# Half of a modulation group on VectorE, three modulation groups by halves at three norms, and VectorE's tiles loaded by GpSimd

## The chip, the cores and the metric

The kernel runs on one core of a Trainium2 chip. The metric is the device time of one execution in microseconds (us); the median of the runs of a kernel stands for it. A core has five engines that run their own instruction streams in order: TensorE (PE: matmuls), VectorE (DVE), ScalarE (ACT), GpSimd (POOL) and SyncE (SP). They wait for each other by semaphores. Transfers are issued from a queue of SP, ACT or POOL and are moved by 16 DMA engines. In a timeline a row of an issue stands under SPq, ACTq or POOL.

## The reference

Two blocks follow each other on 512 latent tokens of width 1024 (and 256 context tokens in the first block). The first block has two layers; each is modulated by six vectors for the latents and six for the context, which come from a condition `c` by one product with `ada_w`:

```python
sc_lat, sc_ctx = jax.nn.silu(c), jax.nn.silu(c_ctx)
for i in range(2):
    mod_l = (sc_lat @ ada_w[i] + ada_b[i])[:, None, :]
    mod_c = sc_ctx @ ada_w[i] + ada_b[i]
    sh1_l, s1_l, g1_l, sh2_l, s2_l, g2_l = jnp.split(mod_l, 6, axis=-1)   # mod_c alike
    h = rms_norm(x, norm1_g[i]) * (1 + s1) + sh1
    x = x + g1 * mixer(h)          # i = 0: gated linear attention; i = 1: neighbourhood attention
    h = rms_norm(x, norm2_g[i]) * (1 + s2) + sh2
    x = x + g2 * conv_ffn(h)       # i = 1: the latents alone
x = second_block(rms_norm(x_lat, final_g))
```

The second block (two layers of three attention branches and an MLP) isn't touched by the change.

## The kernel before

**Modulation groups.** The twelve vectors of the two layers are computed in six groups of two vectors, 0 to 5, each for latents and context at once; a group is a product of 2 x 1024 (the silu of the conditions, `scT`) with 1024 x 2048 weights (`ada_w`, 8 MB in f32). Each group is needed at its own time: group 0 at the very start, group 1 for the output projection of the gated attention and the first feed-forward's norm, group 2 for that norm's scales and the feed-forward's output, 3 and 4 for the second layer's attention, 5 for the second layer's feed-forward.

There are two ways of computing a group. `gada` (L355) takes PE: 16 steps (eight slices of 128 rows, two halves of 1024 columns), each loads 512 KB into a tile `aw` and multiplies it in two matmuls of 512 columns with the 32 columns of `scT` as the stationary operand, so that the four blocks of 512 columns land in four groups of 32 partitions of the tile `ad`. At its end a DVE transpose and a sum with the bias give `mod`. `vada` (L386) takes DVE: it loads tiles `at` of 128 x 512 (256 KB, two buffers), multiplies each by a scalar for each partition and adds it to an accumulator `aa` (one operation for the latents, one for the context; L406 for the first slice, L408 for the others), and PE sums over the partitions at the end of each half with a matrix `unit` (L416).

Before the change: group 0 by its own function on PE in the start; 1 and 2 by `gada` in the gated attention, as a side work that is dealt out one step for each 2.5 units of planned main work (`AEV`), loads on SP's queue through four buffers; 3 and 4 by `vada` in the first feed-forward, loads on SP's queue; 5 by `gada` in two pieces at the first and the second norm, where PE waits for a norm anyway, loads on ACT's queue through seven buffers (`ADA5`: two steps ahead of each norm, six behind it).

**Stages.** The start loads the tokens and sums their squares over the features (`sumsq`: ACT squares, DVE adds, L479), which gives 1/rms (`rstd`: a matmul with ones, L351, then two ACT operations). `modulate0` (L514) then makes `hh` (on ACT) and the low part `hl` (DVE subtracts `hh` from `E`, which POOL makes, L521). All main products are three matmuls of rounded high and low parts (`mm3`: L330, L332, L334). The first projections follow, then v (L639 to L641), then four heads of the gated attention; PE is given projections of the next head between the parts of a head. The output projection and the first norm (`token_rstd`, `modulate`) come next, the first feed-forward (`ffn`), the second norm, the neighbourhood attention (`na`) with its output projection, the third norm and the second feed-forward.

**What sets the order.** The code is written in program order with generators: `weave` and `mixed` (L229, L241) deal out steps of side work by planned costs. A scheduler then places the instructions of each engine in a fixed stream by its own estimate of when each can run; it may move an instruction ahead of ones that were written earlier. On the chip each engine runs that stream in order and waits at the head of it. A tile with n buffers can be loaded anew only when the readers of the n-th tile before it are done.

## Time and profile before

| | us |
|---|---|
| median of 3 runs | 3698.85 (3698.39 to 3700.05) |
| profiled execution | 3697.38 |
| its span | 3695.6 |
| PE busy | 3617.4 (98%) |
| DVE busy | 2175.7 (59%) |
| ACT busy | 1434.2 (39%) |
| POOL busy | 361.7 (10%) |

The span runs from the first to the last instruction of the profiled execution. The windows that the rows use are: the start up to the first v projection at 60.64, from there to the first level of head 0 at 84.87, and three heads from first product of a head to that of the next (84.87, 186.75, 286.58, 371.85). The first norm lies at 496 to 512, the second at 1076 to 1085, the third at 1452 to 1460.

### The profile page before, as it was taken

The page shows a single profiled execution, that of the slowest core. Times are in us where ns is not written, and L with a number is a line of the kernel's source. Part 1 is how long each engine was busy: PE and PEld are TensorE (multiplying, and loading weights), DVE is VectorE, ACT ScalarE, POOL GpSimd, SP SyncE. Part 2 cuts the span into 40 slices and gives each one's busy share as a digit, 9 for nine tenths or more (in the row PEclk, how much of TensorE's full clock was granted, in tenths as well). Part 3 has the DMA queues.
Part 4 walks back from the last instruction along what each step waited for, and adds up shares of the span by engine and source line. Part 5 has one row for each costly group of instructions (what it writes and reads, how often), then busy time and mean ns, then how long its engine had stood idle before and what let it go on. Part 6 is the DMA issues. An engine that isn't in the chain of part 4 may idle for free.

```text
span 3695.6 us, 48674 instructions
## 1 busy us (share of the span) xinstructions
PE 3617.4 (98%) x19296; PEld 2972.7 (80%) x19296; DVE 2175.7 (59%) x3471; ACT 1434.2 (39%) x2199; POOL 361.7 (10%) x342
## 2 busy tenths in 40 slices
PE   7999999999999998999999999999999999999998
PEld 5778878888878886888787877888888787788888
DVE  5566776364355776444766775544456687644446
ACT  4334432121344454333546534422234653432223
POOL 2000000000001110000210121210121012121011
PEclk9999999999999999999999999999999999999999
DMA  6332343232112222323322232323332223233323
GB/s 254 123 95 66 120 151 107 71 117 83 60 62 58 52 57 66 99 95 99 116 82 87 92 102 80 120 97 97 97 119 82 91 89 104 81 120 98 97 94 118
DMA packets 128931, 360.21 MB, mean 97 GB/s; under 512 B 31664, under 2 KB 33968, under 8 KB 128704
## 3 DMA queue, kind: packets, MB, share of 16 engines
q1 hardware_dynamic: 97632, 321.70, 27.1%
q10 hardware_dynamic: 28928, 27.47, 2.6%
q0 software_dynamic: 2144, 7.93, 0.6%
q8 instruction: 152, 2.49, 0.3%
q14 instruction: 75, 0.61, 0.1%
HBM read 342.10 MB, written 8.65 MB: 95 GB/s over the span
## 4 chain that ended last, share of the span: by engine, by line
PE 45%; DVE 3%; issue 1%; ACT 1%; POOL 0%; DMA 0%; SPq 0%; DVEq 0%; POOLq 0%; ACTq 0%
PE mm L330 13%; PE mm L334 13%; PE mm L332 13%; PE yp L1335 1%; DVE wlo L320 1%; PE yp L1426 1%; PE mm L1238 1%; PE ma L1495 1%; PE mm L1240 0%; PE mm L1239 0%; PE ma L1414 0%; DMA tf<-s 0%; POOL ta L1483 0%; DVE ta L1478 0%; PE ma L1398 0%
## 5 line engine op out<-in xcount | busy, mean ns | idle before, releaser
L319 ACT ACTIVATE whi<-wst 128x1024 fp32r<-128x1024 f32 (+3 forms) x519 | 544.1, 1049 | 1335.8 <-PE mm L332 1113.5
L320 DVE TENSOR_TENSOR wlo<-wst,whi 128x1024 fp32r<-128x1024 f32 (+3 forms) x519 | 690.0, 1330 | 270.6 <-ACT whi L319 264.8
L330 PE MATMUL mm<-xh,whi 128*128 128x512 f32 x1664 | 664.4, 400 | 6.1 <-DVE ta L1124 3.0
L332 PE MATMUL mm<-xl,whi 128*128 128x512 f32 x1664 | 651.1, 391 | 1.6 <-DVE xl L1153 1.6
L334 PE MATMUL mm<-xh,wlo 128*128 128x512 f32 x1664 | 650.4, 391 | 0.0
L330 PE MATMUL mm<-ty,whi 128*128 128x512 f32 (+1 forms) x1008 | 381.1, 378 | 0.1
L334 PE MATMUL mm<-ty,wlo 128*128 128x512 f32 (+1 forms) x1008 | 378.9, 376 | 0.0
L330 PEld LDWEIGHTS mm<-xh,whi 128*128 128x128 f32 x1664 | 313.5, 188 | 79.7 <-issue 15.4
L334 PEld LDWEIGHTS mm<-xh,wlo 128*128 128x128 f32 x1664 | 313.0, 188 | 69.0 <-issue 2.1
L332 PEld LDWEIGHTS mm<-xl,whi 128*128 128x128 f32 x1664 | 313.6, 188 | 62.6 <-DVE xl L1153 2.0
L330 PE MATMUL mm<-hh,whi 128*128 128x256 f32 (+2 forms) x1176 | 339.6, 352 | 7.7 <-ACT hh L510 2.9
L332 PE MATMUL mm<-hl,whi 128*128 128x256 f32 (+2 forms) x1176 | 333.2, 347 | 0.7 <-DVE hl L524 0.4
L334 PE MATMUL mm<-hh,wlo 128*128 128x256 f32 (+2 forms) x1176 | 331.2, 345 | 1.7 <-DVE wlo L320 1.7
L332 PE MATMUL mm<-ta,whi 128*128 128x512 f32 (+1 forms) x752 | 279.1, 371 | 0.4 <-DVE ta L325 0.4
L330 PEld LDWEIGHTS mm<-hh,whi 128*128 128x128 f32 (+1 forms) x1176 | 189.2, 189 | 56.7 <-issue 21.0
L330 PEld LDWEIGHTS mm<-ty,whi 128*128 128x128 f32 x1008 | 189.7, 188 | 37.6 <-issue 4.2
L334 PEld LDWEIGHTS mm<-ty,wlo 128*128 128x128 f32 x1008 | 189.6, 188 | 37.0 <-issue 2.6
L334 PEld LDWEIGHTS mm<-hh,wlo 128*128 128x128 f32 (+1 forms) x1176 | 189.8, 188 | 31.1 <-DVE wlo L320 2.7
L332 PEld LDWEIGHTS mm<-hl,whi 128*128 128x128 f32 (+1 forms) x1176 | 189.0, 188 | 27.8 <-DVE hl L508 1.8
L332 PEld LDWEIGHTS mm<-ta,whi 128*128 128x128 f32 x752 | 141.7, 188 | 25.1 <-DVE ta L325 0.6
L1681 DVE TENSOR_TENSOR x<-x,mm 128x512 f32<-128x512 f32 x56 | 38.5, 687 | 172.1 <-PE mm L334 172.1
L869 DVE SCALAR_TENSOR_TENSOR x<-mm,mod,x 128x512 f32<-128x512 f32 x52 | 38.9, 749 | 164.7 <-PE mm L334 164.7
(427 smaller groups left out, 5920.4 us busy)
## 6 DMA issues: line engine op xcount, KB each, us to landing
wst<-w_in SPq DMA_DIRECT2D x100, 512.0 KB, 3.4
wst<-ffn_in SPq DMA_DIRECT2D x88, 512.0 KB, 3.4
wst<-w_dn SPq DMA_DIRECT2D x70, 512.0 KB, 3.4
wst<-w_up SPq DMA_DIRECT2D x64, 512.0 KB, 3.4
aw<-ada_w SPq DMA_DIRECT2D x40, 512.0 KB, 5.1
at<-ada_w SPq DMA_DIRECT2D x64, 256.0 KB, 3.2
wst<-w_v SPq DMA_DIRECT2D x32, 512.0 KB, 3.4
wst<-ffn_out SPq DMA_DIRECT2D x32, 448.0 KB, 3.3
```

The costliest lines, as they stand in the source:

```text
L319: nc.scalar.activation(out=hi[:, :n], in_=st[:, :n], func=AF.Copy)
L320: nc.vector.tensor_tensor(out=lo[:, :n], in0=st[:, :n], in1=hi[:, :n].bitcast(F32), op=ALU.subtract)
L330: nc.tensor.matmul(o, whi, xh, start=first, stop=False)
L332: nc.tensor.matmul(o, whi, xl, start=False, stop=False)
L334: self.after = nc.tensor.matmul(o, wlo, xh, start=False, stop=last)
L869: nc.vector.scalar_tensor_tensor(out=x[:, n, a:b], in0=o[:, :b - a], scalar=gsc, in1=x[:, n, a:b], op0=ALU.mult, op1=ALU.add)
L1238: nc.tensor.matmul(o, a, wh[:, ws], start=(k == 0), stop=False)
L1335: nc.tensor.matmul(yp[64 * e:64 * e + 64, sb * P:], v[h // 4][:, sb, c:c + 64], a, start=(sb == 0), stop=True, skip_group_check=True)
L1426: nc.tensor.matmul(yp[64 * e:64 * e + 64, b * P:b * P + P], vm[p // 2][:, c, c0:c0 + 64], T[:, c * P:c * P + P], start=(c == 0), stop=(c = ...
L1495: nc.tensor.matmul(z[:, (s2 - s) * P:], wt, part, start=False, stop=True, skip_group_check=True)
L1681: nc.vector.tensor_tensor(out=x[:, n, :], in0=x[:, n, :], in1=o, op=ALU.add)
```

## The change

Group 2 leaves the gated attention's PE work: its first half (2, 0) goes to DVE by `vada` as the first item of that side work, its second half (2, 1) to the first norm. Group 5 goes by halves to the second norm (5, 0) and to the third norm (5, 1), which had none. The new function `gadah` computes half a group on PE in matmuls of 256 columns on four groups of partitions; at the third norm its tiles are four buffers of `bm` (used by the attention before), loaded in pieces of 256 KB by POOL's queue, and a hook in `token_rstd` puts six of its steps behind the sum of squares, the rest behind the norm. `vada` takes a list of halves, loads by POOL's queue, and sums over the partitions in eight matmuls of 256 columns on four groups instead of four of 512 on two. The weights' layout follows. Group 1 stays in the gated attention behind (2, 0), dealt out one step for each 4.4 units.

```diff
-AEV = 2.5
+AEV = 4.4
...
-    def vada(self, sg, pool):
+    def vada(self, pool, parts, dst):
...
+        steps = [(sg, v, kc, c) for sg, v in parts for kc in range(KD) for c in range(2)]
+
+        def load(sg, v, kc, c):
             t = self.sb(pool, [P, 512], "at", 2)
-            o = 1024 * half + 512 * c
-            nc.sync.dma_start(out=t, in_=io["ada_w"][sg - 1, kc, :, o:o + 512])
+            o = 1024 * v + 512 * c
+            nc.gpsimd.dma_start(out=t, in_=io["ada_w"][sg - 1, kc, :, o:o + 512])
             return t
...
-                ps, R = self.mm(), slice(64 * half, 64 * half + 64)
+                ps = self.mm()[:, :256]
                 for r in range(2):
-                    for g in range(2):
-                        o = 64 * half + 32 * g
-                        nc.tensor.matmul(ps[o:o + 32, :], self.unit[:, r, :], acc[r][:, 512 * g:512 * g + 512],
+                    for g in range(4):
+                        nc.tensor.matmul(ps[32 * g:32 * g + 32, :], self.unit[:, r, :], acc[r][:, 256 * g:256 * g + 256],
                                          start=(r == 0), stop=(r == 1), skip_group_check=True)
...
+    def gadah(self, sg, v, width, lag, tile, queue, bank):
+        nc, io = self.nc, self.io
+        steps = [(kc, o) for kc in range(KD) for o in range(0, 1024, width)]
+        st = []
+        for i in range(len(steps) + lag):
+            if i < len(steps):
+                kc, o = steps[i]
+                t = tile()
+                queue.dma_start(out=t, in_=io["ada_w"][sg - 1, kc, :, 1024 * v + o:1024 * v + o + width])
+                st.append(t)
+            if i == lag - 1:
+                yield 0.0
+                ps = bank()[:, :256]
+            if i >= lag:
+                kc, o = steps[i - lag]
+                for c in range(0, width, 256):
+                    g = (o + c) // 256
+                    i2 = nc.tensor.matmul(ps[32 * g:32 * g + 32, :], self.scT[:, kc, :], st[i - lag][:, c:c + 256],
+                                          start=(kc == 0), stop=(kc == KD - 1), skip_group_check=True)
+                    self.order(i2, self.after)
+                yield 0.45
...
+        d = tile()[:, :256]
+        nc.vector.transpose(out=d, in_=ps)
...
-    def token_rstd(self, pool, x, parts, tags, ps=None):
+    def token_rstd(self, pool, x, parts, tags, ps=None, hook=lambda: None):
...
         acc = self.sumsq(pool, x, KD, parts, tags)
+        hook()
...
         def ada():
-            for sg in range(1, 3):
-                yield from self.gada(sg, pool, (("aw", AW),), AW - 1)
+            yield from self.vada(pool, ((2, 0),), ("at", 2))
+            yield from self.gada(1, pool, (("aw", AW),), AW - 1)
...
-                ada = net.gada(5, F, (("aw", 7),), 7, nc.scalar)
+                aw = lambda: net.sb(F, [P, 1024], "aw", 7)
+                ad = lambda: net.ps.tile([P, 512], F32, tag="ad", bufs=1, name="ad")
+                ada = net.gadah(2, 1, 1024, 7, aw, nc.scalar, ad)
...
-                rs = norm(*ADA5[:2])
+                rs = norm(ada, *ADA5[:2])
+                drain(ada)
+                ada = net.gadah(5, 0, 1024, 7, aw, nc.scalar, ad)
+                next(ada)
...
-                        (None for sg in (3, 4) for _ in net.vada(sg, F)))
+                        net.vada(F, ((3, 0), (3, 1), (4, 0), (4, 1)), ("at", 2)))
...
                     net.na(hh, hl, yh, yl, N)
+                    half = lambda: net.sb(N, [P, 7, 8, 16], "bm", 4).rearrange("p d i j -> p (d i j)")[:, :512]
+                    ada = net.gadah(5, 1, 512, 4, half, nc.gpsimd,
+                                    lambda: net.ps.tile([P, 512], F32, tag="sc", bufs=1, name="sc"))
+                    next(ada)
                     net.block1_out("na_wo", KD, lambda k: yh[:, k], lambda k: yl[:, k], x2, 4, 0, [(0, NL, 0)], perm=x2)
...
-                    rs = net.token_rstd(N, x2, [(0, NL)], dict(acc=("P", 3), rs=("rsb", 1), sq=("T", 4), keep=X))
+                    rs = net.token_rstd(N, x2, [(0, NL)], dict(acc=("P", 3), rs=("rsb", 1), sq=("T", 4), keep=X),
+                                        hook=lambda: [next(ada, None) for _ in range(6)])
+                    drain(ada)
```

The streams of the engines show where the scheduler puts this. DVE in the start, before: `A` collects the sums of squares (seven adds), `gl` holds the square of a slice of the tokens or a transposed piece of group 0, `gs` the gains.

```order
L1206 TENSOR_TENSOR fgm<-vecs 128x8
L479 TENSOR_TENSOR A<-A,gl 128x768 x7
L449 STREAM_TRANSPOSE gl<-ad 128x128
L453 TENSOR_TENSOR mod_167<-gl,vecs 128x2x4
L455 SCALAR_TENSOR_TENSOR gs_168<-mod_167,vecs 128x4
```

The same place after:

```order
L1237 TENSOR_TENSOR fgm<-vecs 128x8
L405 TENSOR_SCALAR aa<-at,scT 128x512 x4
L509 TENSOR_TENSOR A<-A,gl 128x768
L407 SCALAR_TENSOR_TENSOR aa<-at,scT,aa 128x512
L509 TENSOR_TENSOR A<-A,gl 128x768
```

The first four operations of (2, 0) stand ahead of the first sum, one more between any two of the seven sums; the other 22 follow among the work of `modulate0`, the last five of them right ahead of the low part of the weights that the v projection needs, and all 32 stand ahead of the first rotation of q and k.

POOL in the start, before: the loads of constants, a library, then the `E` of `modulate0`.

```order
L531 DMA cst<-con 128x261
L532 DMA vecs<-vecs 128x372
L521 ISA
L521 TENSOR_SCALAR E<-F,gs_168,mod_167 128x256
L521 TENSOR_SCALAR E<-F,gs_168,mod_167 128x512
```

After:

```order
L562 DMA cst<-con 128x261
L563 DMA vecs<-vecs 128x372
L394 DMA at<-ada_w 128x512 x8
L552 ISA
L552 TENSOR_SCALAR E<-F,gs_168,mod_167 128x256
L552 TENSOR_SCALAR E<-F,gs_168,mod_167 128x512
```

Eight of the sixteen loads of (2, 0) stand ahead of the first `E`, three ahead of the `E` of `y`, three ahead of those of `sr`, two behind them.

PE in the gated attention, before (`E` and `s` are a level of a head, `hh`, `hl` the next head's projection):

```order
L334 MATMUL mm<-hh,wlo 128x512
L334 MATMUL mm<-hh,wlo 128x256
L373 MATMUL ad<-aw,scT 32x512
L738 MATMUL s_945<-E 128x128 x6
L373 MATMUL ad<-aw,scT 32x512
L330 MATMUL mm<-hh,whi 128x512
```

After, in the same stage:

```order
L335 MATMUL mm<-hh,wlo 128x512
L335 MATMUL mm<-hh,wlo 128x256
L416 MATMUL mm<-aa,unit 32x256 x8
L374 MATMUL ad<-aw,scT 32x512 x3
L769 MATMUL s_1734<-E 128x128 x6
```

The 64 modulation matmuls stood in 33 places, most of them one or two at a time; the 32 that are left stand in nine, as x10 ahead of head 0, then x3 (behind the unit matmuls), x3, x1, x4, x7, x1, x1 and x2.

The third norm: DVE before, from the last sum of squares (`P`) to the modulated slices (`ta`, `xl`).

```order
L866 SCALAR_TENSOR_TENSOR x_3452<-mm,mod_5731,x_3452 128x8x16 x4
L320 TENSOR_TENSOR wlo<-wst,whi 128x1024
L479 TENSOR_TENSOR P<-P,T 128x512
L498 SCALAR_TENSOR_TENSOR ta<-x_3452,gs_12368,rsb 128x512 x3
L511 SCALAR_TENSOR_TENSOR xl<-ta,mod_5731,xh 128x512 x3
```

DVE after:

```order
L897 SCALAR_TENSOR_TENSOR x_3462<-mm,mod_6340,x_3462 128x8x16 x4
L321 TENSOR_TENSOR wlo<-wst,whi 128x1024
L509 TENSOR_TENSOR P<-P,T 128x512
L449 STREAM_TRANSPOSE bm<-sc 128x256
L451 TENSOR_TENSOR mod_8491<-bm,vecs 128x16
L529 SCALAR_TENSOR_TENSOR ta<-x_3462,gs_12498,rsb 128x512 x3
```

And PE after (`mm<-P,cst` is the row of ones of the norm):

```order
L335 MATMUL mm<-nyh,wlo 128x512
L442 MATMUL sc<-bm,scT 32x256 x8
L352 MATMUL mm<-P,cst 128x512
L442 MATMUL sc<-bm,scT 32x256 x24
L331 MATMUL mm<-xh,whi 128x512 x3
```

The half group's matmuls stand on both sides of the row of ones, and its transpose and bias on DVE ahead of the first modulated slice; from there to the end the streams are the same as before.

## Rows read from the trace of the kernel before

**Rows 1.** The page: busy time of each engine, share of the span, instructions.

```profile
PE 3617.4 (98%) x19296; PEld 2972.7 (80%) x19296; DVE 2175.7 (59%) x3471; ACT 1434.2 (39%) x2199; POOL 361.7 (10%) x342
```

**Rows 2.** Windows: stretch, length, busy time (instructions) by engine, PEclk, DMA share, GB/s.

```profile
20.00:40.00 20.00, 16.75 (x171) 10.62 (x170) 13.88 (x20) 9.21 (x15) 9.20 (x8) 0.74 1.00 385
...
60.64:84.87 24.23, 22.66 (x162) 16.54 (x161) 10.98 (x16) 12.03 (x19) 2.41 (x1) 0.93 0.73 239
84.87:186.75 101.88, 101.83 (x626) 77.02 (x625) 59.31 (x77) 39.65 (x48) 2.88 (x2) 1.00 0.36 113
186.75:286.58 99.83, 99.77 (x640) 79.02 (x638) 61.00 (x81) 40.78 (x48) 2.89 (x2) 1.00 0.31 97
286.58:371.85 85.27, 84.27 (x586) 76.00 (x585) 60.19 (x80) 41.13 (x49) 3.00 (x2) 1.00 0.19 58
```

**Rows 3.** DMA issues: out<-in, queue, count, KB each, median us to landing.

```profile
aw<-ada_w SPq DMA_DIRECT2D x40, 512.0 KB, 5.1
at<-ada_w SPq DMA_DIRECT2D x64, 256.0 KB, 3.2
...
xd<-x POOLq DMA_DIRECT2D x16, 256.0 KB, 2.3
...
out<-v POOLq DMA_DIRECT2D x4, 256.0 KB, 2.9
out<-v SPq DMA_DIRECT2D x4, 256.0 KB, 2.2
...
vecs<-vecs POOLq DMA_DIRECT2D x1, 186.0 KB, 7.0
```

**Rows 4.** Timeline of the start: us, duration, engine, line, operation [idle before <-releaser].

```profile
10.79 6.27 DVE L479 TENSOR_TENSOR A<-A,gl 128x768 f32<-128x768 f32 x6 [0.77 <-ACT gl L477]
...
26.44 0.97 DVE L524 TENSOR_TENSOR hl<-E,hh 128x768 fp32r<-128x768 f32 x1 [1.05 <-POOL E L521]
...
52.51 0.96 DVE L524 TENSOR_TENSOR hl<-E,hh 128x768 fp32r<-128x768 f32 x1 [0.68 <-POOL E L521]
...
60.64 0.28 PE L639 MATMUL mm<-whi,hh 128*128 128x256 f32 x1
```

**Rows 5.** Single lines: L408 of vada, and POOL's issues of xd.

```profile
L408 DVE SCALAR_TENSOR_TENSOR aa<-at,scT,aa x112: 741/747/755, 461.3 to 852.4; 128x512 f32<-128x512 f32 x112
...
L1216 POOL DMA_DIRECT2D xd<-x x16: 540/553/583, 1834.9 to 2755.3; - x16
```

**Rows 6.** Windows of the modulation matmuls (L373) alone, the stretches of Rows 2.

```profile
60.64:84.87 24.23, 6.16 (x28) 0.79 (x28) 0.93 0.73 239
84.87:186.75 101.88, 17.85 (x56) 2.41 (x56) 1.00 0.36 113
186.75:286.58 99.83, 13.65 (x44) 1.85 (x44) 1.00 0.31 97
```

**Rows 7.** Timeline at the first norm.

```profile
500.26 1.06 PE L373 MATMUL ad<-aw,scT 128*32 128x512 f32 x8 [3.91 <-issue]
...
506.93 4.03 ACTq L364 DMA_DIRECT2D aw<-ada_w  x6
...
511.01 3.14 ACT L510 ACTIVATE hh<-cv,mod 128x256 fp32r<-128x256 f32 x6 [4.64 <-issue]
...
512.18 1.01 PE L330 MATMUL mm<-hh,whi 128*128 128x512 f32 x2 [2.89 <-ACT hh L510]
```

**Rows 8.** Timeline of PE at a unit cluster of the first feed-forward.

```profile
590.26 1.91 PE L416 MATMUL mm<-aa,unit 128*32 128x512 f32 x8
```

**Rows 9.** Timeline at the third norm.

```profile
1452.17 0.39 PE L334 MATMUL mm<-nyh,wlo 128*128 128x512 f32 x1
...
1454.77 0.68 DVE L479 TENSOR_TENSOR P<-P,T 128x512 f32<-128x512 f32 x1
...
1458.11 2.08 DVE L498 SCALAR_TENSOR_TENSOR ta<-x,gs,rsb 128x512 f32<-128x512 f32 x3 [2.66 <-ACT rsb L301]
...
1459.73 1.65 PE L330 MATMUL mm<-xh,whi 128*128 128x512 f32 x3 [3.04 <-ACT xh L510]
```

More of the change, by code (lines that the diff above doesn't have):

```diff
@@ L164, in _lay_out @@
             else:
-                aw.append(s.transpose(0, 1, 4, 2, 3, 5).reshape(KD, P, 2048))
+                s = s.transpose(0, 1, 2, 4, 3, 5) if len(aw) >= 1 else s.transpose(0, 1, 4, 2, 3, 5)
+                aw.append(s.reshape(KD, P, 2048))
             ab.append(np.concatenate([b[va], b[vb]], 0).T)
@@ new lines, in vada @@
+                b = self.vec("ada_b", 16 * sg + 8 * v, 8).unsqueeze(2).to_broadcast([P, 8, 2])
+                nc.vector.tensor_tensor(out=self.mod[sg][:, 8 * v:8 * v + 8, :], in1=b, op=ALU.add,
+                                        in0=d.rearrange("p (j r) -> p j r", r=32)[:, :, 0:2])
+                yield 0.0
+    def gadah(self, sg, v, width, lag, tile, queue, bank):
[9 more added lines that the diff above has]
+            if i == lag - 1:
+                yield 0.0
+                ps = bank()[:, :256]
[7 more added lines that the diff above has]
+                yield 0.45
+        if sg not in self.mod:
+            self.mod[sg] = self.C.tile([P, 16, 2], F32, name=f"mod{sg}")
+        d = tile()[:, :256]
+        nc.vector.transpose(out=d, in_=ps)
+        b = self.vec("ada_b", 16 * sg + 8 * v, 8).unsqueeze(2).to_broadcast([P, 8, 2])
+        nc.vector.tensor_tensor(out=self.mod[sg][:, 8 * v:8 * v + 8, :], in1=b, op=ALU.add,
+                                in0=d.rearrange("p (j r) -> p j r", r=32)[:, :, 0:2])
@@ L884, in proj @@
                          k == 0, k == KD - 1)
-            next(side, None)
-            next(side, None)
+            for _ in range(2):
+                next(side, None)
             return outs
@@ L1790, in emit, with norm @@
                 net.ps = f.enter_context(tc.tile_pool(name="psum2", bufs=1, space=PSUM))
-                def norm(before, after):
+                def norm(ada, before, after):
                     for _ in range(before):
```

17 lines of the change are left out of this document (5 added, 12 removed).

## The prediction

> **What bounds the kernel now.** I read the page's busy shares first, then the windows of the stretches that the change touches, then the timeline inside them. TensorE (PE) is busy 98% of the span [rows 1], so work on it counts almost in full, and work on another engine counts only where PE waits for it. There are two kinds of stretch. In the heads of the gated attention PE is full: heads 1 and 2 take 101.88 and 99.83 us and hold modulation matmuls, head 3 takes 85.27 and holds none, PE being busy 84.27 of it [rows 2]. At the start and at the norms PE waits for a chain through VectorE (DVE), ScalarE and GpSimd (POOL). The start also has no spare transfers: from 20 to 40 us the DMA engines are busy all the time, at 385 GB/s [rows 2].
>
> The sum is made on the profiled execution (3697.4 us, 1.8 of it outside the span); the median of three is 1.5 above it, and I add that at the end. A measurement of this kernel can tell some 0.2% (7.4 us) from no change.
>
> **What the gated attention gives back.** Before, 32 steps of modulation (two fp32 matmuls each; the trace has two records for each) lie in it: 14 in head 1, 11 in head 2, 7 ahead of them [rows 6]. They cost 101.88 + 99.83 - 2 x 85.27 = 31.2 us in the heads, that is 1.19 and 1.32 a step, and 6.2 busy and about 1 of waits ahead of them: 38.4. After, 16 steps are left, and they stand closer together. The order has them as x10, x3, x3, x1, x4, x7, x1, x1, x2 matmuls. Where two steps stand together, the pair has a row: 1.06, or 0.27 a matmul [rows 7]. The 24 matmuls in x10, x4, x7 and the first x3 are then 6.4 us; the other eight stand in five places at the 1.2 to 1.3 that a lone step costs, about 6. The clusters x10 and x7 need five and four tiles from four buffers, so each waits for a load or two: of the 5.1 us to landing [rows 3] I take half, twice, 5. The eight unit matmuls are 1. Sum 18.4, gain **-20**. If the clusters don't wait, -25; if every step left costs 1.25 and the unit cluster 1.9, -15.
>
> **What the opening costs.** The order puts all 32 DVE operations of the half (2,0) ahead of the first rotation of q and k, that is, into the start and not into the attention. The first four, which need tiles 0 and 1, even stand ahead of the first sum of squares, and one more stands in each of the gaps between the seven sums. DVE goes in order, so each sum waits for a tile. Sixteen tiles pass through two buffers: a buffer's next load is issued when DVE has read it twice (0.75 each [rows 5]), costs POOL some 0.6 to issue [rows 5], and lands L later. On POOL eight of these loads stand ahead of the first E of the modulation, three, three and two behind later ones.
> By hand from the durations in the rows, with L = 3.9: tiles 0 and 1, queued behind vecs (issued at 2.0, landed 7.0 later [rows 3]), arrive at about 11 and 12.5; tiles 2, 3 and 4 feed the gaps between the sums, and the last sum ends at 25.6 where it was 17.06 [rows 4]. The first E then waits for the loads of tiles 5 to 7, whose buffers are free only after the second use of tile 5, which itself stands behind the first gains: the first hl ends at 42.6 instead of 27.4, the last at 67.3 instead of 53.5 [rows 4]. Behind it stand five more operations of the half and the wlo that the v projection needs: it starts at 74.6 instead of 60.64 [rows 4], **+14**. The same walk gives +7.7 at L = 2.3, +9.8 at 2.9, +17.5 at 4.5 and +21.7 at 5.2.
>
> No row shows a load from memory by POOL's queue in a quiet stretch. The nearest: at by SP's queue lands in 3.2; POOL's stores of the same 256 KB land in 2.3 (xd) and 2.9 (out), and out by SP's queue in 2.2 [rows 3]. So POOL's queue adds 0.7 on the same tensor, and 3.2 + 0.7 = 3.9 is my value. The bounds are 2.3, the quickest row, and 5.2, the landing of aw by SP while much else was queued [rows 3].
>
> **The norms.** At the first norm ScalarE now issues its loads behind three of the modulated slices and not ahead of all; before, they held it 4.64 and PE waited 2.89 for it [rows 7]. But seven loads that wait for buffers still stand ahead of the fourth slice, so PE starts one slice early and waits again: -1 (-2.5 to +2, since the tiles of the next DVE part stand ahead of the last residual sums). The second norm keeps its form: 0.
> The third norm had no modulation matmuls. Now 16 steps pass through four buffers of bm. Four tiles are there when the output projection ends; the other twelve are three round trips of landing, 0.55 of POOL's issue and about 0.5 of matmul. PE has 24 of the matmuls between the row of ones and the first xh, and DVE has the transpose and the sum of the bias ahead of the first ta. From the end of the projection (1452.6) the last step ends 15.9 later at L = 3.9, and with 0.6 for the two DVE operations ta starts 10.8 later than the 1458.11 of before [rows 9]: **+10.8**; PE's wait for xh of 3.04 [rows 9] becomes a wait for tiles. At L = 2.3 it is +6.0, at 4.5 +12.6, at 5.2 +14.7.
>
> **The unit matmuls in the first feed-forward.** Four clusters of 1.91 us [rows 8] on two column groups become four on four groups with half the columns each: -0.95 apiece, **-3.6** (-4 to 0). The loads of these parts change queue; DVE has slack there (59% [rows 1]), so I cost that at nothing. If the cover is gone it shows as PE waiting for a DVE result in that feed-forward.
>
> **Sum:** -20 + 14 - 1 + 10.8 - 3.6 = +0.2, so 3697.6 for a profiled execution and **3699** for the median.
>
> **Rivals.**
> *Quick landings (faster).* POOL's queue lands a load as quickly as the store xd, 2.3 [rows 3]: opening +7.7, third norm +6.0, with -24.6 from the rest: -10.9, **3688**. For it: xd's 16 stores all land in 2.3 while DVE works. Against it: it is a store, in a quiet stretch. It passes -7.4 for L under 2.9. The Trainium skill, DMA: Bandwidth & Descriptors, "Anatomy of one DMA — SWDGE (gpsimd) path", gives about 2.0 us and bytes over 436 GB/s for one transfer on this path, by which 256 KB would land in some 2.6 us (an estimate); the sum by it would be about -9. The stores out and xd agree with it, and no run here shows it for a load yet.
> *Slow landings (slower).* In the opening, where the DMA engines are full [rows 2], and in the third norm, where weights are loaded beside it, a load takes about 5: opening +20.5, third norm +13 to +14, sum +9.4, **3708**. It is slower by over 0.2% from L = 4.7 on. For it: vecs, a smaller load on this queue, took 7.0 in the opening [rows 3]. Against it: vecs was queued behind cst and beside the input loads. The Trainium skill, SBUF — State Buffer, in its warning on the "DVE blocks DMA" trap, says that while VectorE runs an operation that takes both shared ports GpSimd can't write descriptors, and that a transfer of 620 ns then takes 3100: that speaks against this change, whose loads are issued beside DVE work. Here POOL's sixteen issues of xd took 540 to 583 ns [rows 5], in a part where DVE works too, so I give it no term; with 2.5 more for each issue in the chains it would give this rival's time or more.
> *The heads don't get shorter.* DVE becomes the bound of the heads, so only 10 of the 20 come back: +10, 3709. Against it: head 3, without modulation, ran at 85.27 with DVE busy 60.19 [rows 2], and the order puts no DVE work of the half into the heads. Part of the slower case.
> That the half does not lie in the gated attention at all, as the change is named, is in the order and in the sum already.
>
> **How the numbers follow.** Forecast (within 0.2%) 0.42. Faster 0.30: quick landings 0.22, and a larger gain in the heads with middling landings 0.08. Slower 0.28: slow landings 0.22, the heads 0.06. The range must reach both rivals, whose chances together are over a half: from quick landings with a point to spare, 3686, to slow landings with some of the bounds above, 3711.
>
> **What would show it.** The last sum of squares near 25.6 with DVE waiting for at; the first v projection near 75; heads 1 and 2 together near 181 to 186; the first ta of the third norm some 11 later after the projection than before, with PE waiting for bm; unit clusters of about 1. The median landing of at and bm decides between the cases: under 2.9, between, or over 4.7. The prediction is wrong if these loads don't set the two chains, or if the modulation matmuls left in the heads cost as much as those that were there.

## The result, and the profile after

The changed kernel takes 3720.92 us (median), the kernel before 3698.85 when both are measured side by side: a ratio of 1.0053, 95% interval 1.0039 to 1.0066. It is **slower by 0.5%**. The forecast was 3699 with a range to 3711, so the range missed by 10 us. The nearest rivals are the one of heads that don't get shorter, 3709, and the one of slow landings, 3708. One more execution, in which the mean granted clock was 0.911, took 3791.28 and is not part of the ratio.

The profiled execution took 3713.53, span 3711.8: the quickest of the executions; others lie at 3720 to 3724. So there are two questions: where 16.2 us come from (3711.8 against 3695.6, trace against trace), and where the other 7 to 10 do. Both are answered below, the second by experiment 9.

The page of the changed kernel, busy time by engine (compare [rows 1]):

```profile
PE 3604.2 (97%) x19408; PEld 2978.7 (80%) x19408; DVE 2194.7 (59%) x3507; ACT 1435.0 (39%) x2199; POOL 422.1 (11%) x438
```

TensorE (PE) does 13.2 us less work and the span is 16.2 longer: PE waits 29 us more. The modulation work did leave PE. What replaced it is waiting.

To find where, I took each matmul that both streams hold and subtracted its start before from its start after. Times count from the first instruction of each execution. Each difference between two rows of this table is what the stretch in between cost or gave. The heads are counted from 0 here; the prediction's heads 1, 2 and 3 are 0, 1 and 2.

| place in PE's stream (us before) | shift after |
|---|---|
| first projection of the start, `hh` (24.4) | +10.6 |
| first matmul of the v projection (60.64) | +19.4 |
| head 0 (84.87) | +18.3 |
| head 1 (186.75) | -1.2 |
| head 2 (286.58) | -13.8 |
| head 3 (371.85) | -8.8 |
| ahead of norm 1 (496) | -4.4 |
| behind norm 1 (512) | -2.1 |
| end of the first feed-forward (1076) | +0.6 |
| behind norm 2 (1085) | +1.8 |
| ahead of norm 3 (1452) | +1.8 |
| behind norm 3 (1459.73) | +15.9 |
| end | +16.2 |

Windows of the changed kernel: 20 to 40 us, then v projection to head 0, and the three periods between heads 0, 1, 2 and 3, the stretches of [rows 2] (length, busy us and instructions of PE, PEld, DVE, ACT, POOL, granted clock, DMA share, GB/s):

```profile
20.00:40.00 20.00, 11.45 (x158) 6.69 (x154) 16.99 (x26) 9.44 (x14) 7.87 (x7) 0.83 0.95 361
80.02:103.18 23.16, 19.59 (x166) 16.65 (x165) 12.73 (x17) 12.96 (x20) 2.39 (x1) 1.00 0.61 205
103.18:185.55 82.37, 82.37 (x576) 74.92 (x575) 55.70 (x72) 38.38 (x45) 2.88 (x2) 1.00 0.17 55
185.55:272.77 87.22, 87.15 (x608) 76.02 (x608) 60.91 (x83) 41.33 (x49) 2.89 (x2) 1.00 0.21 70
272.77:363.03 90.26, 88.42 (x602) 75.75 (x601) 60.04 (x79) 40.93 (x49) 2.93 (x2) 1.00 0.25 78
```

From 20 to 40 us PE is busy 11.45 instead of 16.75, and VectorE (DVE) 16.99 instead of 10.62. Heads 0 and 1 are shorter, 82.37 and 87.22 instead of 101.88 and 99.83, and PE is full in them. Head 2 is longer, 90.26 instead of 85.27, since it now holds modulation matmuls.

DVE's timeline in the start (start, duration, what it waited for in brackets), which answers to the seven sums of [rows 4]:

```profile
9.96 0.88 DVE L405 TENSOR_SCALAR aa<-at,scT 128x512 f32<-128x512 f32 x2 [1.11 <-DMA at<-ada_w]
12.05 0.88 DVE L405 TENSOR_SCALAR aa<-at,scT 128x512 f32<-128x512 f32 x2 [1.21 <-DMA at<-ada_w]
12.85 0.95 DVE L509 TENSOR_TENSOR A<-A,gl 128x768 f32<-128x768 f32 x1
16.93 0.75 DVE L407 SCALAR_TENSOR_TENSOR aa<-at,scT,aa 128x512 f32<-128x512 f32 x1 [3.13 <-DMA at<-ada_w]
17.60 0.95 DVE L509 TENSOR_TENSOR A<-A,gl 128x768 f32<-128x768 f32 x1
...
25.23 0.75 DVE L407 SCALAR_TENSOR_TENSOR aa<-at,scT,aa 128x512 f32<-128x512 f32 x1 [2.08 <-DMA at<-ada_w]
...
27.43 0.95 DVE L509 TENSOR_TENSOR A<-A,gl 128x768 f32<-128x768 f32 x1
...
65.60 1.42 DVE L407 SCALAR_TENSOR_TENSOR aa<-at,scT,aa 128x512 f32<-128x512 f32 x2 [1.65 <-DMA at<-ada_w]
...
78.04 1.41 DVE L407 SCALAR_TENSOR_TENSOR aa<-at,scT,aa 128x512 f32<-128x512 f32 x2 [0.52 <-DMA at<-ada_w]
79.37 1.22 DVE L321 TENSOR_TENSOR wlo<-wst,whi 128x1024 fp32r<-128x1024 f32 x1
```

The sums stand between the half's operations, and behind operations that wait for tiles: the last ends at 28.38 (27.43 + 0.95) instead of 17.06. All 32 operations of the half lie between 9.96 and the `wlo` of 79.37, which the v projection waits for; it starts at 80.02 instead of 60.64. Between 9 and 80 us DVE waits for a tile `at` nine times, 14.0 us in all. The landings of `at` in that stretch are 3.2 at least, 5.1 in the median and 8.9 at most. Over the whole kernel the median is 3.5 and that of `bm` 3.7 (DMA issues: out<-in, queue, count, KB, median us to landing; compare [rows 3]):

```profile
at<-ada_w POOLq DMA_DIRECT2D x80, 256.0 KB, 3.5
...
bm<-ada_w POOLq DMA_DIRECT2D x16, 256.0 KB, 3.7
```

Timeline of the changed kernel at norm 1 (compare [rows 7]):

```profile
500.29 0.75 DVE L407 SCALAR_TENSOR_TENSOR aa<-at,scT,aa 128x512 f32<-128x512 f32 x1 [2.47 <-DMA at<-ada_w]
500.96 0.75 DVE L900 SCALAR_TENSOR_TENSOR x<-s,mod,x 128x512 f32<-128x512 f32 x1
...
502.31 1.93 PE L442 MATMUL ad<-aw,scT 128*32 128x256 f32 x16 [10.42 <-issue]
...
508.68 0.51 ACT L541 ACTIVATE hh<-cv,mod 128x256 fp32r<-128x256 f32 x1 [0.25 <-DVE cv L529]
```

ScalarE no longer holds the first slice `hh` (0.25 of waiting where it was 4.64), as the prediction said. But the last residual sum, L900, stands behind an operation of `vada` that waits 2.47 for its tile, and PE's modulation cluster starts at 502.31 instead of 500.26 (at a shift of -4.4 there). Before, that sum stood at 498.91:

```profile
498.91 0.75 DVE L869 SCALAR_TENSOR_TENSOR x<-s,mod,x 128x512 f32<-128x512 f32 x1
```

The seven loads still hold ScalarE ahead of the fourth slice of `hh`, until 514.17, but PE waits only 0.6 us for that slice, since it has the products of the first slices to do.

Timeline at norm 3, where before the row of ones was followed at 1458.11 by `ta` and at 1459.73 by the first matmul with `xh` [rows 9]:

```profile
1454.30 1.07 PE L442 MATMUL sc<-bm,scT 128*32 128x256 f32 x16
...
1455.24 1.07 POOL L433 DMA_DIRECT2D bm<-ada_w  x2 [48.75 <-PE sc L442]
...
1458.58 0.62 PE L442 MATMUL sc<-bm,scT 128*32 128x256 f32 x4
...
1462.00 1.75 PE L442 MATMUL sc<-bm,scT 128*32 128x256 f32 x12 [1.60 <-DMA bm<-ada_w]
...
1466.61 2.27 PE L442 MATMUL sc<-bm,scT 128*32 128x256 f32 x12 [1.48 <-DMA bm<-ada_w]
...
1471.78 1.25 PE L442 MATMUL sc<-bm,scT 128*32 128x256 f32 x8 [1.47 <-DMA bm<-ada_w]
1473.07 0.45 DVE L449 STREAM_TRANSPOSE bm<-sc 128x256 f32<-128x256 f32 x1 [15.80 <-PE sc L442]
...
1473.96 2.08 DVE L529 SCALAR_TENSOR_TENSOR ta<-x,gs,rsb 128x512 f32<-128x512 f32 x3 [0.22 <-DVE mod L451]
```

Four records are one step. The first four steps run at 1454.30; the other twelve go through the four buffers in three rounds, until 1473.03. The first `xh` matmul follows at 1475.64. From the last matmul of the projection to it there are 21.7 us, where there were 7.6.

The unit matmuls, as a group of the first feed-forward (count, busy us, mean ns; of the two kernels, before first):

```profile
L416 PE MATMUL mm<-aa,unit 128*32 128x512 f32 x32 | 7.6, 598 | 0.0
```

```profile
L416 PE MATMUL mm<-aa,unit 128*32 128x256 f32 x64 | 4.3, 385 | 0.0
```

That is -3.3, and the shifts at the four clusters add to -3.4.

### The profile page after: what moved, and what is told of

Read it like the earlier page. It is cut to its first block, busy times and chain, and to the rows that moved or that the text cites. A ratio compares the mean times of both kernels' runs of the same rounds, so it can differ in the third digit from the quotient of the medians.

```text
span 3711.8 us, 49002 instructions
## 1 busy us (share of the span) xinstructions
PE 3604.2 (97%) x19408; PEld 2978.7 (80%) x19408; DVE 2194.7 (59%) x3507; ACT 1435.0 (39%) x2199; POOL 422.1 (11%) x438
## 4 chain that ended last, share of the span: by engine, by line
PE 44%; DVE 3%; issue 1%; DMA 1%; ACT 1%; POOL 0%; SPq 0%; DVEq 0%; ACTq 0%; POOLq 0%
PE mm L331 13%; PE mm L335 12%; PE mm L333 12%; PE yp L1366 1%; PE mm L1269 1%; DVE wlo L321 1%; PE yp L1457 1%; PE mm L1270 1%; PE mm L1271 1%; PE ma L1526 1%; DMA tf<-s 1%; PE ma L1445 0%; SPq L1590 0%; PE ma L1429 0%; PE ma L1428 0%
## 5 line engine op out<-in xcount | busy, mean ns | idle before, releaser
L331 PEld LDWEIGHTS mm<-xh,whi 128*128 128x128 f32 x1664 | 313.4, 188 | 79.1 <-issue 15.4
L331 PE MATMUL mm<-hh,whi 128*128 128x512 f32 (+2 forms) x1176 | 339.1, 352 | 5.4 <-ACT hh L551 3.1
L333 PE MATMUL mm<-hl,whi 128*128 128x512 f32 (+2 forms) x1176 | 335.8, 349 | 6.7 <-DVE hl L555 6.1
L335 PE MATMUL mm<-hh,wlo 128*128 128x512 f32 (+2 forms) x1176 | 332.6, 347 | 5.0 <-DVE wlo L321 5.0
L900 DVE SCALAR_TENSOR_TENSOR x<-mm,mod,x 128x512 f32<-128x512 f32 x52 | 38.9, 749 | 165.0 <-PE mm L335 165.0
```

What stands on the lines that cost most here:

```text
L331: nc.tensor.matmul(o, whi, xh, start=first, stop=False)
L333: nc.tensor.matmul(o, whi, xl, start=False, stop=False)
L335: self.after = nc.tensor.matmul(o, wlo, xh, start=False, stop=last)
L900: nc.vector.scalar_tensor_tensor(out=x[:, n, a:b], in0=o[:, :b - a], scalar=gsc, in1=x[:, n, a:b], op0=ALU.mult, op1=ALU.add)
```

## The experiments

The theory behind the prediction was that waits for tiles set two chains (start and norm 3). What it left open, and what the runs had to tell apart: whether the start lost its time to waiting or to DVE's work; whether the queue or the place of the half was the cause; whether the half would have been free in the heads; and, later, why executions of one kernel differ by 10 us. Shifts are against the kernel before, by the same places as in the table. Ratios compare with the kernel before on the same chip.

**1. The half's loads behind the start.** The loads of (2, 0) are ordered behind POOL's first operation of the rotation of q and k; the queue stays.

```diff
-            nc.gpsimd.dma_start(out=t, in_=io["ada_w"][sg - 1, kc, :, o:o + 512])
+            i = nc.gpsimd.dma_start(out=t, in_=io["ada_w"][sg - 1, kc, :, o:o + 512])
+            self.order(i, self.rot)
...
-            nc.gpsimd.tensor_tensor(out=sw, in0=sw, in1=sn, op=ALU.mult)
+            self.rot = nc.gpsimd.tensor_tensor(out=sw, in0=sw, in1=sn, op=ALU.mult)
```

> The changed kernel with one order more: the loads of the half (2, 0) stand on GpSimd behind the first rotation of q and k, so none of its VectorE operations lies in the start. Theory 1 (in the start VectorE waits in order for tiles that GpSimd's queue lands in 5.1 us): the first v projection starts at 60.6 again instead of 80.0, the heads take up the 24 us of VectorE work at little cost (at most 4), and the execution is 15 to 20 shorter than the changed kernel's profiled 3713.5, so 3694 to 3698. Theory 2 (the half costs its time wherever it stands, since the heads have no VectorE time to spare once modulation matmuls are gone): the start is back but the heads grow by 10 to 20, the total stays at 3705 to 3713.

Measured: 3710.54, ratio 1.0025 (1.0015 to 1.0034). The v projection is back at -0.6, so the whole 19.4 of the start came from the half standing there. But the stretch from there to norm 1 gives only 13 instead of 24: shift ahead of norm 1 -13.8, where the changed kernel had -4.4. PE's waits in that stretch (60 to 380 us; total, times, longest) show part of it:

```profile
PE mm L335 <- DVE wlo L321: 4.5, 3, 2.7
PE ad L374 <- DMA aw<-ada_w: 3.3, 1, 3.3
PE s L795 <- DVE S L800: 1.9, 2, 1.1
```

So the half isn't free in the heads either: DVE's work there is near enough to the bound that PE waits for `wlo` and for `S`. Of the 20 that the start cost, 11 are lost again, and the total lies in theory 2's range. Its words, that the half costs its time wherever it stands, hold by half.

**2. The old queue.** All loads of `vada` by SyncE's queue (SP), nothing else.

```diff
-            nc.gpsimd.dma_start(out=t, in_=io["ada_w"][sg - 1, kc, :, o:o + 512])
+            nc.sync.dma_start(out=t, in_=io["ada_w"][sg - 1, kc, :, o:o + 512])
```

> The changed kernel with all of VectorE's tiles loaded by SyncE's queue, as before the change. The scheduler then puts the half (2, 0) behind the start: 15 of its 32 operations between the end of the start and the first rotation. Theory 1 (the queue is what let the half be drawn into the start, and VectorE's wait there is the loss): the last sum of squares ends near 17 again, and the first v projection starts within 3 of 60.6. In the first feed-forward, where I cost the change of queue at nothing: the wait of 2.5 ahead of the last residual sum of the first norm (0.8 more than before) falls by less than 1. Theory 2 (the loss comes from the added 4 MB in a start whose transfers are full): the first v projection stays over 70, since the same tiles are still loaded early.

Measured: 3701.24, ratio 1.0005 (0.9996 to 1.0015), some 20 less than the changed kernel. The scheduler places the half behind the start by itself: v projection +0.2. So **the change of queue is what put the half into the start**: POOL's queue was idle there, and loads on it were placed early, with DVE's work behind them; on SP's queue they stand behind the weights. What SP's queue costs is one wait of PE, for `aw`, which now stands behind four loads `at` that wait for buffers. PE's and SP's timelines of this run:

```profile
79.00 1.92 PE L374 MATMUL ad<-aw,scT 128*32 128x512 f32 x4 [9.04 <-DMA aw<-ada_w]
```

```profile
62.38 11.44 SPq L394 DMA_DIRECT2D at<-ada_w  x4
73.91 0.86 SPq L365 DMA_DIRECT2D aw<-ada_w  x2
```

Head 0 stands at +7.2 for it, norm 1 is reached at -14.8, and norm 1 itself is -1.2, though the wait ahead of the last residual sum is only 0.5 shorter (2.00). Norm 3 costs 15.1, much as in the changed kernel.

**3. Norm 3 without modulation.** The half (5, 1) becomes a fifth half of `vada` in the first feed-forward; the `gadah` of norm 3 and its hook go.

```diff
-                        net.vada(F, ((3, 0), (3, 1), (4, 0), (4, 1)), ("at", 2)))
+                        net.vada(F, ((3, 0), (3, 1), (4, 0), (4, 1), (5, 1)), ("at", 2)))
...
-                    half = lambda: net.sb(N, [P, 7, 8, 16], "bm", 4).rearrange("p d i j -> p (d i j)")[:, :512]
-                    ada = net.gadah(5, 1, 512, 4, half, nc.gpsimd,
-                                    lambda: net.ps.tile([P, 512], F32, tag="sc", bufs=1, name="sc"))
-                    next(ada)
...
-                                        hook=lambda: [next(ada, None) for _ in range(6)])
-                    drain(ada)
```

> The changed kernel with the half (5, 1) as a fifth half of VectorE's work in the first feed-forward; the third norm has no modulation matmuls again. Theory 1 (the third norm pays for three and more round trips of tiles through four buffers): from the last matmul of the projection to the first xh it takes 7.6 again instead of 21.7, and the execution is 13 to 14 shorter than the changed kernel, near 3700; the fifth half costs one unit cluster more (1.3) in the feed-forward. Theory 2 (the feed-forward has no room for a fifth half on VectorE): PE waits there for VectorE and the gain is under 8.

Measured: 3710.51, ratio 1.0025 (1.0015 to 1.0035). Norm 3 costs 0.0 (+6.3 on both sides of it), so its 14 were the half's alone. In the feed-forward the fifth half costs about 5 net against the changed kernel, so the gain is 10 and not 14.

**4. Waiting or work.** Only two tiles of (2, 0) are loaded and used for all sixteen steps; the sums of that half are not the reference's. DVE's 32 operations stay.

```diff
-            t = self.sb(pool, [P, 512], "at", 2)
+            t = self.sb(pool, [P, 512], "at", 2) if sg != 2 or len(kept) < 2 else None
...
+            if sg == 2:
+                if len(kept) == 2:
+                    return kept[c]
+                kept.append(t)
```

> The changed kernel with two loads of the half (2, 0) in place of sixteen: its VectorE operations stay in the start but read the first two tiles again and again (the sums of that half are left out in this sense, so its values are not those of the reference). Theory 1 (waiting for tiles is the loss): the last sum of squares ends near 22 (seven sums and twelve of the operations behind the first tiles at 10 to 12.5), the first v projection starts at 62 to 67. Theory 2 (the 24 us of VectorE work in the way is the loss, whatever the tiles do): it starts at 72 or later.

Measured in one run: 3707.78. The last sum ends at 24.1 and the v projection starts at 69.6, a shift of +9.0: between what the two theories expected. DVE's timeline of this run shows why the sums are still late:

```profile
13.96 0.95 DVE L515 TENSOR_TENSOR A<-A,gl 128x768 f32<-128x768 f32 x1
14.83 0.74 DVE L413 SCALAR_TENSOR_TENSOR aa<-at,scT,aa 128x512 f32<-128x512 f32 x1
15.49 0.95 DVE L515 TENSOR_TENSOR A<-A,gl 128x768 f32<-128x768 f32 x1
```

Between the sums nothing waits, but each stands behind an operation of 0.74, and six operations stand ahead of the first. Of the 19.4 about 9 are DVE's work in the way, and about 10 go with the fourteen loads that this run leaves out. Most of these 10 should be DVE's waits for tiles (14.0 us in the changed kernel), but the run doesn't separate them from what the loads take from other transfers: the first weights `aw` of group 0, issued at about 5 in each kernel, land at 14.3 before, 16.2 here and 17.1 in the changed kernel.

**5. Old queue and norm 3 free** (the edits of 2 and 3 together).

> e2_sync and e3_no51 together: VectorE's tiles by SyncE's queue, the half (5, 1) as a fifth half in the first feed-forward, the third norm without modulation matmuls. Theory 1 (the losses lie in the start and in the third norm and add up stage by stage): e2_sync's 3701 less the 15 of the third norm, plus 3 to 6 for the fifth half, so 3689 to 3692, faster than before by 0.2 to 0.3%. Theory 2 (what a stage gives back is lost again in the next ones, in PE's pace or clock): 3696 or more.

Measured: 3688.02, ratio 0.9969 (0.9957 to 0.998). The stages add: ahead of norm 1 -13.8, at 1076 -13.6, over norm 3 0.0. So the change without these two losses is worth some 11 us.

**6. The same, with group 1 ahead of the half** (PE's steps first, so that `aw` isn't queued behind `at`).

```diff
-            yield from self.vada(pool, ((2, 0),), ("at", 2))
             yield from self.gada(1, pool, (("aw", AW),), AW - 1)
+            yield from self.vada(pool, ((2, 0),), ("at", 2))
```

> As f1_sync_no51, with group 1 (matmuls) ahead of the half (2, 0) (VectorE) in the side work of the gated attention. In e2_sync PE waits 9.0 once for a tile aw, ahead of head 0: SyncE's queue holds it behind tiles at, which wait for their buffers. Theory 1 (that wait is a loss): it goes, head 0 starts 5 to 7 earlier than in e2_sync, and the execution is 3 to 7 shorter than f1_sync_no51. Theory 2 (the heads are then held by VectorE, which gets the same work later): no difference, within 2.

Measured: **3684.47**, ratio 0.9963 (0.995 to 0.9977): this version is 0.4% faster than the kernel before. The longest wait for `aw` is 2.1 instead of 9.0, but head 0 comes only 2.9 earlier than in 5: the same matmuls of group 1 now stand ahead of head 0. The gain of 3.5 on 5 is within the width of their intervals.

**7. Norm 3's tiles by SP's queue.**

```diff
-                    ada = net.gadah(5, 1, 512, 4, half, nc.gpsimd,
+                    ada = net.gadah(5, 1, 512, 4, half, nc.sync,
```

> The changed kernel with the tiles of (5, 1) loaded by SyncE's queue at the third norm. From the last matmul of the projection to the first xh it takes 21.7 in the changed kernel and 7.6 before. Theory 1 (round trips through four buffers set it): each of the three to four rounds gets 0.5 to 0.9 shorter, so 18 to 20. Theory 2 (GpSimd's queue is what is slow): under 14.

Measured in one run: 3721.36. From the last projection matmul to the first `xh` 23.6 us, where the changed kernel has 21.7 and neither theory had more than 20. The landings are 3.0, 4.0 and 5.0 (least, median, most), so POOL's queue is not what is slow. PE's clock was lower there (the row of ones took 2.08 instead of 1.10), so a small gain could be hidden.

**8. Norm 3 with twelve tiles ahead.** Eight buffers of q and k, free by then, are added to the four of `bm`; the lag is 12.

```diff
-                    half = lambda: net.sb(N, [P, 7, 8, 16], "bm", 4).rearrange("p d i j -> p (d i j)")[:, :512]
-                    ada = net.gadah(5, 1, 512, 4, half, nc.gpsimd,
+                    spare = iter([("q", [P, NL], 4)] * 4 + [("k", [P, NT], 4)] * 4)
+
+                    def half():
+                        tag, shape, bufs = next(spare, ("bm", [P, 7, 8, 16], 4))
+                        if tag == "bm":
+                            return net.sb(N, shape, tag, bufs).rearrange("p d i j -> p (d i j)")[:, :512]
+                        return net.sb(N, shape, tag, bufs, F32R).bitcast(F32)[:, :512]
+
+                    ada = net.gadah(5, 1, 512, 12, half, nc.gpsimd,
```

> The changed kernel with twelve tiles of (5, 1) loaded ahead (eight more, in tiles of the attention that are free by then), so that one round trip is left at the third norm. Theory 1 (round trips set it): from the last matmul of the projection to the first xh 12 to 15 instead of 21.7, the execution 7 to 10 shorter than the changed kernel. Theory 2 (PE's modulation matmuls themselves, at the lower clock of a PE that has waited, set it): 18 or more.

Measured: 3712.86, ratio 1.0037 (1.0023 to 1.005), 8 less than the changed kernel. The stretch at norm 3 is 15.8 instead of 21.7, just above theory 1's 12 to 15. One round of loads is left, and it is what PE waits for:

```profile
1464.22 1.05 PE L442 MATMUL sc<-bm,scT 128*32 128x256 f32 x16
1468.77 3.69 PE L442 MATMUL sc<-bm,scT 128*32 128x256 f32 x16 [3.50 <-DMA bm<-ada_w]
```

Two rounds of three gone gave 5.9, so the rounds set the time at norm 3. That is less than the two rounds took, since the round that is left starts only behind the row of ones (1464.22), where in the changed kernel the first one starts right behind the projection (1454.30).

**9. The changed kernel once more**, unaltered, for a second profile.

> The changed kernel a second time, unaltered, for one more profile. Theory 1 (the 7 us between its profiled execution, 3713.5, and its other executions, about 3721, are TensorE's granted clock in the opening): where this execution takes about 3721, the first head of the attention starts at about 108 to 109 us instead of 103.2, the granted clock from 60 to 112 us is about 0.87 instead of 0.93, and the stretches behind the heads take what they took in the first profile; where it takes 3713, head 0 starts near 103. Theory 2 (the difference lies in the later stages, by the pace at which TensorE issues the same matmuls): head 0 starts near 103 in either case, and an execution of 3721 loses its 7 us between norm 1 and the end.

Measured: 3723.78, span 3722.0, 10.2 more than the first profile. The v projection starts at +18.1, a little earlier than in the first (+19.4), and head 0 at +22.4 instead of +18.3. Windows of the two executions from 70 to 90 us (the column behind POOL's is the granted clock: 1.00 is the upper of its two levels, 2.4 GHz, and 0.50 the lower, 1.2 GHz), the first profile and then the second:

```profile
70.00:75.00 5.00, 3.75 (x12) 2.95 (x13) 3.46 (x4) 0.18 (x1) 3.58 (x5) 0.55 0.15 42
75.00:80.00 5.00, 5.00 (x24) 4.09 (x23) 3.38 (x5) 2.24 (x4) 0.22 (x1) 0.77 0.23 68
80.00:85.00 5.00, 4.65 (x46) 4.19 (x45) 1.81 (x2) 2.56 (x7) 0.00 (x0) 1.00 0.60 181
85.00:90.00 5.00, 4.01 (x34) 2.37 (x33) 0.93 (x1) 5.00 (x8) 2.39 (x1) 1.00 0.30 69
```

```profile
70.00:75.00 5.00, 3.81 (x13) 3.16 (x14) 3.77 (x5) 0.00 (x0) 2.77 (x3) 0.68 0.17 52
75.00:80.00 5.00, 3.99 (x23) 3.11 (x21) 3.96 (x5) 3.48 (x8) 0.00 (x0) 0.98 0.18 52
80.00:85.00 5.00, 4.99 (x37) 4.63 (x38) 1.23 (x1) 2.23 (x6) 0.00 (x0) 0.70 0.74 205
85.00:90.00 5.00, 5.00 (x32) 4.57 (x35) 0.68 (x1) 4.92 (x7) 2.39 (x1) 0.62 0.04 10
```

The same instructions, in the same order. In the first execution the clock is low at 70 to 80, where the v projection has to wait for the last tiles in any case, and full behind that; in the second it is low at 70 to 75, recovers, and is low again at 80 to 90, on the v projection and the work ahead of head 0, where PE did 69 instructions (37 + 32) instead of 80. Experiments 7 and 8, whose streams are the same as the changed kernel's up to norm 3, have +23.9 and +23.2 at head 0, and a mean clock of 0.87 from 60 to 112 us, as this run has, where the first profile has 0.93. Theory 1 holds for this part: 4.0 of the 10.2, or 5.3 counted from the v projection. It does not hold for the rest: 1.8 more at norm 1, 1.8 in the first feed-forward, about 1 at norm 3 and about 2 near 1830 us.

**10. The queue alone**: the kernel before, with its 64 loads of `vada` (groups 3 and 4) on POOL's queue.

```diff
-            nc.sync.dma_start(out=t, in_=io["ada_w"][sg - 1, kc, :, o:o + 512])
+            nc.gpsimd.dma_start(out=t, in_=io["ada_w"][sg - 1, kc, :, o:o + 512])
```

> One part alone: the kernel before with vada's 64 loads (groups 3 and 4, first feed-forward) issued by GpSimd's queue instead of SyncE's; nothing else is edited. Theory 1 (the queue costs only where it lets the scheduler place DVE work or loads ahead of a chain): in the kernel before, no half is in the start, so the opening, the heads and norm 3 stay within 0.5 us; at norm 1 the order puts one DVE step of vada less ahead of the last residual sums than before, so norm 1 is -1 to +1 and the whole within 0.2% of before (3695 to 3703). Theory 2 (GpSimd's queue itself holds norm 1 and the unit's feed-forward up, as the 3.5 us between the changed kernel with it and without it at norm 1 suggested): norm 1 +2 to +4, the feed-forward 0 to +3, the whole 3701 to 3706.

Measured: 3706.82, ratio 1.0023 (1.0012 to 1.0035). Norm 1 costs +3.7 (from -1.1 ahead of it to +2.6), the feed-forward nothing (-0.9): theory 2 at norm 1, and the whole just above its range. DVE's timeline of this run shows the mechanism:

```profile
501.79 0.75 DVE L408 SCALAR_TENSOR_TENSOR aa<-at,scT,aa 128x512 f32<-128x512 f32 x1 [2.45 <-DMA at<-ada_w]
502.46 0.74 DVE L869 SCALAR_TENSOR_TENSOR x<-s,mod,x 128x512 f32<-128x512 f32 x1
```

The order has one step of `vada` less ahead of the last residual sum than before, and the sum still comes later, since its tile does. Another 3.6 of this profile's +6 lies near 1830 us, where PE waits 2.9 and 2.0 for DVE and the granted clock is 0.50 for 10 us; nothing was edited there, and experiment 9 has some of it too.

## Why the prediction was wrong, step by step

Trace against trace, what was predicted and what was measured:

| term | predicted | measured |
|---|---|---|
| opening (to the v projection) | +14 | +19.4 |
| gated attention (to norm 1) | -20 | -23.8 |
| norm 1 | -1 | +2.4 |
| first feed-forward | -3.6 | +2.7 |
| norm 2 and up to norm 3 | 0 | +1.2 |
| norm 3 | +10.8 | +14.1 |
| sum (to behind norm 3) | +0.2 | +16.0 |

The largest misses are the first feed-forward (+6.3) and the opening (+5.4), then norm 1 (+3.4) and norm 3 (+3.3); the attention makes up for 3.8 of them.

**The opening: right mechanism, landing mis-sized.** The walk was right in what it said would happen: sums behind tiles, the `wlo` of the v projection behind the last of the half. The step that failed is the 3.9 us for a landing, put together from quiet rows. The measured median in that stretch is 5.1, and the walk at 5.2 had given +21.7, at 4.5 +17.5: +19.4 lies where it should. It is one draw: four other profiles with the same opening (experiments 3, 7, 8 and 9) have +19.7, +16.3, +15.4 and +18.1, all above the +14, at medians of 4.9 to 5.3. The prediction had itself shown that the DMA engines are full there [rows 2] and then took the quiet value. In the quiet parts a load on POOL's queue lands in 3.5, near the 3.9. The Trainium skill's page "DMA: Bandwidth & Descriptors", section "Anatomy of one DMA — SWDGE (gpsimd) path", gives some 2.6 by its figures (an estimate); no load on this queue comes below 3.2 here. The rows count from the start of an issue that takes POOL 0.54, so the quickest agree with that figure if it counts from the issue's end; the median does not, and the quick rival falls.

**The gated attention: better than forecast.** PE waits 4.2 us for `aw` from 80 to 380 us, where 5 was allowed; heads 0 to 2 are shorter by 27.1 together (the first two take 169.6, where the prediction named 181 to 186 as the sign), and head 3 with what follows it, to norm 1, is longer by 4.4. The modulation itself cost about what was reckoned: from the first modulation matmul of a place to the next other matmul, PE's timelines have 36.9 in all before (38.4 reckoned) and 18.8 after (18.4 reckoned), which gives 18.1 of the 23.8. The other 5.7 lie outside these places, and no row says where they come from: that the stretch beat the forecast is luck. The prediction's bound of -15 is a slip: by its own figures, 16 steps at 1.25 and 1.9 for the units, it would be -16.5. The rival in which the heads don't shorten is refuted for this kernel, though experiment 1 shows that it would have held by half if the half stood there. The gain was a consequence of the loss: DVE's work was out of the heads because it was in the start.

**Norm 1: wrong sign.** ScalarE's release came as said. The range of +2 for tiles ahead of the last residual sums was the right worry, and the step that failed is that the change of queue got no term here: the queue alone costs +3.7 (experiment 10), and with all the rest and the old queue norm 1 is -1.2, -3.2 and -2.7 (experiments 2, 5 and 6). By these differences of single profiles the queue's share in the changed kernel is 3.6 to 5.6.

**The first feed-forward: term right, sum wrong.** The unit matmuls gave the 3.4 (four times 0.95 would be 3.8, where the prediction writes 3.6). The rest of the stretch cost 6. PE gains 0.8 right behind norm 1. It loses 1.8 near 845 us, where it waits for ScalarE and DVE: that is the cover that the prediction took as given when it cost the change of queue at nothing. With the changed `vada` on POOL's queue every profile loses there (1.8 to 3.9); on the old queue none does (experiments 2, 5 and 6), and neither does the kernel before with POOL's queue (experiment 10). The largest part, some 5, is the pace of PE's own stream (last section), which no term held.

**Norm 3: the first round mis-sized.** The landing was right in the median (3.7 against 3.9). The step that failed is the round trip: 3.9 + 0.55 + 0.5 = 4.95 was reckoned for each of three, and the rounds took 7.7, 4.6 and 5.2 (1454.30 to 1462.00, 1466.61 and 1471.78). So the excess of 2.8 lies in the first. There the four buffers come free together; POOL issues the first load 0.94 after the matmuls start (1454.30 to 1455.24) and the third at 1456.52, and the third and the fourth land 5.4 after their issue, beside a load of weights (`wst`, issued at 1456.70, landed after 5.3). The loads of the later rounds land in 3.6 to 3.8, three in a row too. This is what the rival of slow landings said of norm 3, for one round.

**The descriptor trap.** The 80 issues of `at` took 539 ns in the median and 617 at most, most of them beside DVE's work, so giving it no term was right. The Trainium skill's page "SBUF — State Buffer", in its warning on the "DVE blocks DMA" trap, ties it to operations of VectorE in a two-port mode. No row shows which operations here run in one, so this trace neither bears the warning out nor refutes it.

**The other 7 us.** They are in none of the terms. Experiment 9 puts 4.0 of its 10.2 down to a lower granted clock between the v projection and head 0; the rest is spread over four places of 1 to 2 us, and its cause stays open. That a start with more waits brings more of this was not tested.

## What to carry to other kernels

A load moved to an idle queue is not only issued by another engine: a scheduler may place it, and the work that it feeds, far earlier, into a stretch that can't afford it; look in the order for what stands behind the moved loads before costing the queue. A landing belongs to the stretch where it happens: where the DMA engines are full, take the rows from there (5.1 here), not those from quiet parts (3.5). A round through few buffers costs the release and the queue of issues as well as landing and work, and its loads can meet others (7.7 here against 4.6 and 5.2); the number of rounds is what to cut: from three to one gave 5.9 us.

## What the runs showed of the hardware

**Two paces of one stream.** At a granted clock of 1.00, the same sequence of matmuls of 512 and 256 columns runs at two paces. Groups of the stretch from 640 to 700 us, before and after (count, busy us, mean ns):

```profile
L330 PE MATMUL mm<-yh,whi 128*128 128x512 f32 x48 | 18.9, 394 | 0.0
L332 PE MATMUL mm<-yl,whi 128*128 128x512 f32 x48 | 18.9, 394 | 0.0
L334 PE MATMUL mm<-yh,wlo 128*128 128x512 f32 x47 | 18.5, 394 | 0.0
```

```profile
L333 PE MATMUL mm<-yl,whi 128*128 128x512 f32 x48 | 19.3, 403 | 0.0
L335 PE MATMUL mm<-yh,wlo 128*128 128x512 f32 x48 | 19.1, 398 | 0.0
L331 PE MATMUL mm<-yh,whi 128*128 128x512 f32 x48 | 19.0, 395 | 0.0
```

At the quick pace all three passes take 394 ns; at the other they take 395, 398 and 403. A pair of 512 and 256 columns then comes every 0.353 us instead of 0.347, 1.7% later. The state lasts for tens to hundreds of us: before is quick from 530 to 720 us and slow from 870 to 930, the first profile of the changed kernel the other way round, and its second profile is slow in both (403, 398 and 395 from 880 to 920). So one program has both. It is not chance alone: from 593 to 720 us the ten profiles with the changed first norm and unit matmuls are all slow, and the two with the old stream (before and experiment 10) are quick. It is worth some 5 us in the first feed-forward of the first profile. What sets it is open.

**The lower clock falls at different places in executions of the same program.** In the opening, where PE waits again and again, the clock falls once in the one profile of the changed kernel (70 to 80 us, 0.55 and 0.77) and twice in the other (70 to 75, 0.68, and 80 to 90, 0.70 and 0.62), at a cost of 4 us by the next head. What decides the place is open.
